# A two-layer encoder trunk on one core: work moved from the gap before attention into the values' phase

## The chip, the cores and the metric

The kernel runs on one core of a Trainium2 chip. Its time is device microseconds of one execution. TensorE (PE) multiplies matrices, VectorE (DVE), ScalarE (ACT) and GpSimd (POOL) do the elementwise work, and SyncE (SP) issues nearly all DMA transfers, one after the other and in the order of the program.

## The reference

The input is 1024 rows (frames) of 1024 numbers. Layer 0 mixes the rows with a gated MLP, layer 1 with attention over the own chunk of 64 rows and the eight before it; either ends with a gated feed-forward block. Cut to what this change touches:

```python
h = h + gmlp_mixer(rmsnorm(h, a_norm_g), ...)
h = h + conv_ffn(rmsnorm(h, f_norm_g[0]), ...)            # ffn(0), down(0)
kv = rmsnorm(h, kv_norm_g) @ w_kv                         # keys, values: 16 heads of 64
q = (rmsnorm(h, b_norm_g) @ w_q) * 64 ** -0.5
sc = q . k + rel_bias[clip(i - j)]                        # a chunk sees itself and the 8 chunks before it
o = softmax(sc) @ v
h = h + o @ w_o
h = h + conv_ffn(rmsnorm(h, f_norm_g[1]), ...)
out = rmsnorm(h, final_norm_g)
```

## The kernel before, in words

Everything is float32. An operand is split by a cast on ACT (or DVE) and a subtraction on DVE (or POOL) into a high and a low part, and a product is three matmuls: high by high, high by low, low by high. Large products are done in the Strassen manner: seven products of half-size blocks instead of eight, whose operands are sums of blocks.

The stretch around the change runs like this.

- **down(0)**, the second half of the first feed-forward block, does its seven products in the order 1, 6, 2, 7, 5, 4, 3, each in 11 steps of 12 matmuls; the operands of a step are loaded and split three steps ahead. Beside it, `value_sums` makes what the values need: for each of four k it loads two blocks of the values' weights (tile `vr`), multiplies them by the norm's gain on POOL (L1047, 128x1024 each), forms four block sums on POOL (tile `vS`, L383, 128x512 each) and stores those in DRAM. `aside` says at which step that is called. When products 6 and 7 end, POOL adds them into the residual stream (L960).
- **values()** makes V, again in seven products (1, 2, 3, 6, 7, 5, 4) of four steps m with 12 matmuls (L1139). It takes its weights from DRAM and its results go back there (`vhi`, `vlo`). After products 1 and 3 the queries and keys of the first pair of heads are projected (tile `qk`, L181/184/188), and before the change those results stay in PSUM until V is done.
- **The gap**: then the first pair's q and k are split (`first`), copied by DMA into the tiles that attention reads (`stage`: KM, QE, QS, KS, two rows of 64 partitions each, 12 DMAs for head 0 and 12 for head 1), and `constant_rows` brings constant rows from DRAM through a small tile `e` to the other 64 partitions. `Max` loads the head's bias, forms its row maxima (`mx` matmuls, L1286 and L1293, reduced on DVE at L1289 and L1295) and writes them as one more row into QE (`mr`, L1302 to L1306), so that a score comes out already less its maximum. The first score (`st`, L1332) waits for all of it. Meanwhile PE does START = 75 matmuls of the second pair's projection, the "fills".
- **The heads**: 16 heads by 8 key blocks, a loop of 128 steps s. A step does one block's scores, two blocks of the next head's maxima, the values' product (`po`) of two steps earlier, and some fills, which are the projections of later pairs until step 104, and then the output projection `wo`. `stage` brings the next head's rows.
- **The output projection**: `w_o` weights are loaded at the steps in `loads`; the last pair's result is normalised on DVE, split, and multiplied in.

The order of PE's instructions is written by hand: matmuls advance a clock of the program, and `put_off(us, fn)` issues `fn` when that clock has moved on by so much. The other engines are ordered by a scheduler, except in the first 24 steps of `down`, and each DMA of SP keeps its place in SP's order. An instruction that has to wait holds back what stands behind it on its engine.

## Time and profile before

| | us |
|---|---|
| median of 3 runs (lowest to highest) | 2194.47 (2192.28 to 2202.92) |
| the profiled execution: its time, its span | 2200.13, 2198.4 |
| PE busy | 2124.1 (97% of the span) |
| DVE, ACT, POOL busy | 1591.9, 1075.4, 802.0 (72%, 49%, 36%) |
| mean granted PE clock | 0.984 of full speed |
| values, gap, heads, output projection (from the timeline) | 937 to 1037, to 1087, to 1470, to 1500 |

In the views below, a timeline's row is the start, the duration, the engine, the line of the code, the operation, output<-inputs, and in square brackets the idle time before it and what ended that. L184 is line 184 of the kernel before. A row of the waits is engine, line and what it waited for, then the sum in us, how often, and the longest. A row of the windows gives for a stretch its length and then the busy time (and count of instructions) of PE, PEld, DVE, ACT and POOL, the granted PE clock, the share of the DMA engines and GB/s. Matmuls overlap: a row's duration (0.39 us) is longer than the distance of two starts.

### The profile page before, as it was taken

Reading aid. Unit: us, or ns where it says so; the run is one execution under the profiler, and the core shown is the slowest. Engines: PE = TensorE matmul, PEld = TensorE weight load, DVE = VectorE, ACT = ScalarE, POOL = GpSimd, SP = SyncE. Lnnn points to the kernel's source line nnn. Section 1 sums busy time; section 2 is a strip of 40 time slices with the busy share of each in tenths; the row PEclk is TensorE's granted clock in tenths of the full one; section 3 lists DMA queues with packets and bytes.
Section 4 is the critical chain, followed back from the end, with each engine's and each line's share of the span. In section 5 each row is a group of like instructions: output and inputs, shape, how many; then the busy total and the mean of one; then the engine's idle time right before and its main releaser. Section 6 shows DMA issues by size and latency. Waiting matters only on the chain.

```text
span 2198.4 us, 28916 instructions
## 1 busy us (share of the span) xinstructions
PE 2124.1 (97%) x9832; PEld 1770.0 (81%) x9832; DVE 1591.9 (72%) x2354; ACT 1075.4 (49%) x1879; POOL 802.0 (36%) x560
## 2 busy tenths in 40 slices
PE   9999999999999999999599999889999999999998
PEld 8888878888888878888487888768778888888887
DVE  4197889888888887786255655664888888876676
ACT  6423556454445535544355656542545545454443
POOL 1084743423335552133355544431223332441120
PEclk9999999999999999999799999999999999999999
DMA  7267622545447988444556656834234454579553
GB/s 250 76 211 261 241 78 92 180 142 175 155 152 241 351 296 277 172 134 145 150 130 162 168 136 156 230 115 145 95 110 168 137 185 134 190 245 331 192 188 138
DMA packets 220812, 391.99 MB, mean 178 GB/s; under 512 B 60764, under 2 KB 75484, under 8 KB 220664
## 3 DMA queue, kind: packets, MB, share of 16 engines
q1 hardware_dynamic: 217640, 384.69, 54.6%
q10 hardware_dynamic: 3024, 5.46, 0.7%
q8 instruction: 77, 1.26, 0.2%
q14 instruction: 71, 0.58, 0.1%
HBM read 248.85 MB, written 115.98 MB: 166 GB/s over the span
## 4 chain that ended last, share of the span: by engine, by line
PE 83%; DMA 6%; DVE 6%; issue 2%; POOL 1%; SPq 1%; ACT 1%; DVEq 0%; POOLq 0%; ACTq 0%
PE gate L992 8%; PE up L992 8%; PE up L370 7%; PE up L368 7%; PE up L373 7%; PE gate L373 5%; PE gate L370 5%; PE gate L368 5%; PE vps L503 4%; PE v L1139 3%; PE qkv L188 2%; PE qkv L181 2%; PE qkv L184 2%; PE ups L181 1%; PE ups L184 1%
## 5 line engine op out<-in xcount | busy, mean ns | idle before, releaser
L140 DVE TENSOR_TENSOR wlo<-raw,whi 128x512 fp32r<-128x512 f32 x380 | 349.2, 925 | 139.6 <-ACT whi L139 139.3
L139 ACT CAST whi<-raw 128x512 fp32r<-128x512 f32 x380 | 235.2, 622 | 286.9 <-PE gate L992 180.0
L368 PE MATMUL up<-yh,whi 128*128 128x512 f32 x688 | 268.3, 390 | 3.4 <-ACT whi L139 2.0
L370 PE MATMUL up<-yh,wlo 128*128 128x512 f32 x688 | 268.4, 390 | 0.3 <-DVE wlo L140 0.3
L840 POOL TENSOR_TENSOR h<-a 128x512 f32<-128x512 f32 x44 | 83.9, 1908 | 407.4 <-DVE a L832 394.8
L1346 POOL TENSOR_TENSOR pl<-p,ph 128x640 fp32r<-128x640 f32 (+4 forms) x128 | 159.8, 1251 | 165.2 <-ACT ph L1345 113.1
L370 PE MATMUL gate<-th,wlo 128*128 128x512 f32 x496 | 193.3, 390 | 0.0
L368 PE MATMUL gate<-th,whi 128*128 128x512 f32 x496 | 193.1, 389 | 0.0
L373 PE MATMUL up<-yl,whi 128*128 128x512 f32 x688 | 184.3, 390 | 0.0
L140 DVE TENSOR_TENSOR yl<-raw,yh 128x512 fp32r<-128x512 f32 x172 | 152.4, 888 | 9.0 <-ACT yh L139 9.0
L368 PEld LDWEIGHTS up<-yh,whi 128*128 128x128 f32 x688 | 129.1, 188 | 31.3 <-ACT whi L139 2.4
L370 PEld LDWEIGHTS up<-yh,wlo 128*128 128x128 f32 x688 | 129.3, 188 | 27.6 <-DVE wlo L140 1.1
L373 PEld LDWEIGHTS up<-yl,whi 128*128 128x128 f32 x688 | 129.2, 188 | 27.2 <-POOL yl L140 0.5
L373 PE MATMUL gate<-tl,whi 128*128 128x512 f32 x496 | 132.9, 390 | 0.2 <-DVE tl L140 0.2
L139 ACT CAST whi<-S 128x512 fp32r<-128x512 f32 x160 | 99.1, 619 | 65.8 <-PE up L373 59.8
L140 DVE TENSOR_TENSOR wlo<-S,whi 128x512 fp32r<-128x512 f32 x160 | 129.6, 811 | 0.0
L992 PE MATMUL up<-yl,whi 128*128 128x512 f32 (+1 forms) x312 | 121.7, 390 | 2.0 <-DVE yl L140 1.9
L992 PE MATMUL up<-yh,wlo 128*128 128x512 f32 (+1 forms) x312 | 120.9, 387 | 2.6 <-DVE wlo L140 2.6
L139 ACT CAST yh<-raw 128x512 fp32r<-128x512 f32 x190 | 115.1, 616 | 13.5 <-DMA raw<-gB 8.8
L992 PE MATMUL gate<-yh,wlo 128*128 128x512 f32 (+1 forms) x312 | 121.0, 388 | 0.0
L992 PE MATMUL gate<-yl,whi 128*128 128x512 f32 (+1 forms) x312 | 120.8, 387 | 0.0
L992 PE MATMUL up<-yh,whi 128*128 128x512 f32 (+1 forms) x312 | 120.8, 387 | 0.0
(328 smaller groups left out, 5420.4 us busy)
## 6 DMA issues: line engine op xcount, KB each, us to landing
raw<-in_f_win SPq DMA_DIRECT2D x88, 512.0 KB
gT<-h SPq DMA_DIRECT2D x88, 256.0 KB
h<-in_f_wdown SPq DMA_DIRECT2D x44, 512.0 KB
dS<-h SPq DMA_DIRECT2D x88, 256.0 KB
raw<-dS SPq DMA_DIRECT2D x40, 512.0 KB
raw<-gT SPq DMA_DIRECT2D x40, 512.0 KB
gB<-a SPq DMA_DIRECT2D x66, 256.0 KB
raw<-in_f_wdown SPq DMA_DIRECT2D x30, 512.0 KB
```

Of the source, the lines that this page charges most:

```text
L139: behind[S] = S.copy(hi, src)
L140: return eng.tensor_tensor(lo, src, f32(hi), op=ALU.subtract)
L181: nc.tensor.matmul(ps, wh[:, k, :], xs[k][0], start=k == first, stop=False)
L184: nc.tensor.matmul(ps, wl[:, k, :], xs[k][0], start=False, stop=False)
L368: nc.tensor.matmul(ps, wh[:, k, :], xs[k][0], start=first and k == 0, stop=False, skip_group_check=True)
L370: nc.tensor.matmul(ps, wl[:, k, :], xs[k][0], start=False, stop=False, skip_group_check=True)
L373: nc.tensor.matmul(ps, wh[:, k, :], xs[k][1], start=False, stop=k == 3, skip_group_check=True)
L503: nc.tensor.matmul(ps, a, b, start=k == i == 0, stop=k == KD - 1 and i == 2)
L840: G.tensor_tensor(B[n], x, B.get(y) if isinstance(y, str) else y, op=ALU.subtract)
L992: nc.tensor.matmul(ps[:, cs], w[:, ms], x[:, cs], start=q == i == 0 and p in (1, 6, 5, 4), stop=q == NP - 1 and i == 2, skip_group_check=True)
L1139: nc.tensor.matmul(bank[m], a, b, start=p not in (2, 7) and k == i == 0, stop=k == 3 and i == 2, skip_group_check=True)
L1346: marks[2] = G.tensor_tensor(pl[:, :n], pf[:, :n], f32(ph[:, :n]), op=ALU.subtract)
```

## The change

1. **The gap's work moves into the values' phase.** The first pair's q and k are split as soon as they are projected and written to DRAM (`part`, then 8 DMAs). From there the rows of head 0 are staged: KM and QE (`"me"`) right after each projection, QS and KS (`"s"`) at product 4. Head 0's constant rows are brought in 8 us after the start of the phase by the program's clock, its 15 `mx` matmuls and the row of maxima stand within products 7, 5 and 4 (`first_max`). What stays behind the last value is head 1's staging (12 DMAs) and head 1's constant rows.
2. **START falls from 75 to 56** fills before the first score. The weights of those fills are loaded within the values' phase.
3. **Buffers of the values' phase:** `vt` 4 to 3, `vx` 5 to 3, `vw` 8 to 6, PSUM's two held banks are given up.
4. **`value_sums` later in down(0):** called at steps 46, 53, 60, 67 instead of 28, 37, 46, 55, and POOL takes its multiplications only behind the additions L960.
5. **Bias in two halves** (one for scores, one for maxima), loaded up to a head earlier than before.
6. **Maxima a step sooner** in every head, and their row put off from step 5 instead of 6.
7. **Output projection:** all eight `w_o` weights are on chip before the heads end (two more, at steps 118 and 122, into tiles that are free by then), and the fills behind the last step are 14 instead of 12 per waiting value and reach over m = 7 and 6.

The core of the diff:

```diff
-START = 75
+START = 56
...
                     for x in ((h12,) if p == 6 else (h21, h22)):
-                        G.tensor_tensor(x, x, u, op=ALU.add)
+                        behind["adds"] = G.tensor_tensor(x, x, u, op=ALU.add)
...
-            G.tensor_tensor(rows[j], rows[j], cc[:, c:c + 1].broadcast_to([P, T]), op=ALU.mult)
+            with tc.issue_after(behind["adds"].ins):
+                G.tensor_tensor(rows[j], rows[j], cc[:, c:c + 1].broadcast_to([P, T]), op=ALU.mult)
...
-        down(0, gs, ds, hsave[0], lambda t, acc: norm(h, acc, t, X), {28 + 9 * k: lambda k=k: value_sums(k) for k in range(4)})
+        down(0, gs, ds, hsave[0], lambda t, acc: norm(h, acc, t, X), {46 + 7 * k: lambda k=k: value_sums(k) for k in range(4)})
...
-            if p in (2, 6) and m == 0:
+            if p in (2, 6, 4) and m == 0:
                 yield
...
+    parts = {(0, what): [dp.tile([P, T], F32, name=f"{what}0{n}") for n in ("hi", "lo")] for what in "qk"}
...
+    open_psum(H, 4)
+    with tc.tile_pool(name="vt", bufs=3, reuse_waits="tile") as vt, tc.tile_pool(name="vx", bufs=3, reuse_waits="tile") as vx, \
+            tc.tile_pool(name="vw", bufs=6, reuse_waits="tile") as vw:
+        w2 = {what: weights(0, what) for what in "qk"}
+        put_off(8.0, lambda: constant_rows(0, lambda: npl.tile([P, H], F32, tag="f", name="e")))
+        ys = [None] * 2
+
+        def first_max():
+            place = h_all[1, 1]
+            mx = Max(0, load_bias(1, 0, place[:, 0, 0:2 * P]), place[:, 1, 0:NB], place[:, 1, NB:2 * NB], lambda: mr0,
+                     lambda: place[:, 2, 0:2 * P])
+            for b in range(NB):
+                put_off(3.0 + 1.4 * b, lambda b=b: mx.block(b))
+            put_off(16.0, mx.row)
+
+        for t, _ in enumerate(values()):
+            if t == 2:
+                for hs in halves:
+                    stage(0, hs, "s")
+                continue
+            ys[t] = X["B11"] + X["B21"] if t == 0 else X["B12"] + X["B22"]
+            for what in "qk":
+                ps = psS("qk")
+                proj(ps, w2[what], ys[t])
+                both = [npl.tile([P, H], F32R, tag="acc", name=f"{what}{n}", bufs=4) for n in ("hi", "lo")]
+                part(what, *both, ps)
+                for d, a in zip(parts[0, what], both):
+                    nc.sync.dma_start(d[:, halves[t]], f32(a))
+            stage(0, halves[t], "me")
+            if t:
+                raw1 = new_raw([P, KD, P])
+                w1 = {what: weights(1, what, raw1) for what in "qk"}
+                put_off(12.0, first_max)
+        catch_up()
...
+        put_off(7.0, lambda: constant_rows(1, lambda: b2.tile([P, H], F32, tag="o", name="e")))
         for c in range(2):
-            constant_rows(c, lambda: b2.tile([P, H], F32, tag="o", name="e"))
...
-        mx = Max(0)
-        for b in range(NB):
-            put_off(6.5 + 0.8 * b, lambda b=b: mx.block(b))
-        put_off(14.0, mx.row)
+        bs, bm = {0: new_bias(0, 0)}, {1: new_bias(1, 1)}
...
-        loads = {100: 2, 102: 3, 106: 4, 109: 5, 112: 0, 116: 1}
+        loads = {100: 2, 102: 3, 106: 4, 109: 5, 112: 0, 115: 1, 118: 6, 122: 7}
...
-        mid, end = {2: (1,), 3: (3,), 4: (5,), 5: (7,)}, {1: (0,), 2: (2,), 3: (4,), 4: (6,)}
+        mid, end = {1: (1,), 2: (3,), 3: (5,), 4: (7,)}, {0: (0,), 1: (2,), 2: (4,), 3: (6,)}
...
             if i == LAG + 1 and hd + 1 < NH:
+                bs[hd + 1] = new_bias(0, hd + 1)
+                if hd + 2 < NH:
+                    bm[hd + 2] = new_bias(1, hd + 2)
                 stage_v(hd + 1)
...
-                if i == (6 if p < LAST - 1 else 5):
-                    put_off(0.5 if p < LAST - 1 else 2.0, mx.row)
+                if i == 5:
+                    put_off(0.5, mx.row)
...
-        fill = output([(m, range(LAST - 2, LAST), psS) for m in (2, 3, 4, 5)])
+        two = range(LAST - 2, LAST)
+        fill = output([(7, range(LAST), psS, True), *((m, two, psS, False) for m in (2, 3, 4)), (6, range(LAST), psO, False),
+                       (5, two, psS, False)])
         for h0, b in waiting:
-            for _ in range(12):
+            for _ in range(14):
                 next(fill)
```

Three places show what moves. Lines shift by the change: L1332 before is L1349 after (`st`), L1286 is L1196 (`mx`), L1213 is L1182 (staging), L1182 is L1158 (constant rows).

SP behind the last value before the change: the end of head 1's staging (`km_9394` and so on are head 1's tiles, `thi` and `tlo` the split q and k), the constant rows having been issued between the stagings:

```order
L1182 DMA e<-in_consts 64x512 x2
L1213 DMA km_9394<-thi 64x512
L1213 DMA qe_9392<-thi 64x512
L1213 DMA qs_9393<-thi 64x512
L1213 DMA qs_9393<-tlo 64x512
L1213 DMA ks_9395<-tlo 64x512
L1213 DMA ks_9395<-thi 64x512
L1267 DMA vh_9396<-vhi 128x8x64
L1267 DMA vl_9398<-vlo 128x8x64
L1276 DMA bias<-in_bias 128x512 x2
```

and the same place after, where 12 stagings of head 1 (from `q0hi` and the like in DRAM) begin right behind the last value:

```order
L1182 DMA ks_9469<-k0lo 64x512
L1182 DMA ks_9469<-k0hi 64x512
L1314 DMA vh_9470<-vhi 128x8x64
L1314 DMA vl_9472<-vlo 128x8x64
L1218 DMA bias<-in_bias 128x256 x2
L1158 DMA e<-in_consts 64x512 x2
L1218 DMA bias<-in_bias 128x256 x2
L1314 DMA vh_9471<-vhi 128x8x64
L1314 DMA vl_9473<-vlo 128x8x64
L156 DMA raw<-in_w_kv 128x1024
L1158 DMA e<-in_consts 64x512 x2
```

Head 0's rows have left this place; the two pairs of constant rows `e` that are left are head 1's, and stand behind its staging, two bias loads and V's first loads.

PE between the values and the scores, before (head 0's first maxima among the fills `qkv`):

```order
L184 MATMUL qkv<-yh,wlo 128x512
L181 MATMUL qkv<-yh,whi 128x512
L1286 MATMUL mx<-km_9352,qe_9350 128x128
L184 MATMUL qkv<-yh,wlo 128x512
L181 MATMUL qkv<-yh,whi 128x512
L184 MATMUL qkv<-yh,wlo 128x512
L1286 MATMUL mx<-km_9352,qe_9350 128x256
```

and after, at the end of 56 fills (head 0's first scores, then head 1's first maximum, whose tiles are `km_9468` and `qe_9466`):

```order
L184 MATMUL qkv<-yh,wlo 128x512
L1349 MATMUL st<-qe_8354,km_8356 128x256
L1351 MATMUL st<-qs_8355,ks_8357 128x256
L1349 MATMUL st<-qe_8354,km_8356 128x384
L1351 MATMUL st<-qs_8355,ks_8357 128x384
L181 MATMUL qkv<-yh,whi 128x512
L184 MATMUL qkv<-yh,wlo 128x512
L181 MATMUL qkv<-yh,whi 128x512
L184 MATMUL qkv<-yh,wlo 128x512
L181 MATMUL qkv<-yh,whi 128x512
L1196 MATMUL mx<-km_9468,qe_9466 128x128
```

The scores stand where the maxima stood; the first instruction that reads head 1's constant rows now comes five fills behind the first scores.

POOL in down(0), before (additions L960 between the third and the fourth set of value sums):

```order
L1047 TENSOR_TENSOR vr<-vr,cc 128x1024 x2
L383 TENSOR_TENSOR vS<-vr 128x512
L383 TENSOR_TENSOR vS<-vS,vr 128x512
L383 TENSOR_TENSOR vS<-vr 128x512
L383 TENSOR_TENSOR vS<-vr,vS 128x512
L960 TENSOR_TENSOR h_84<-h_84,u 128x512 x4
L1047 TENSOR_TENSOR vr<-vr,cc 128x1024 x2
```

and after:

```order
L960 TENSOR_TENSOR h_85<-h_85,u 128x512
L960 TENSOR_TENSOR h_86<-h_86,u 128x512
L1047 TENSOR_TENSOR vr<-vr,cc 128x1024 x4
L383 TENSOR_TENSOR vS<-vr 128x512
L383 TENSOR_TENSOR vS<-vS,vr 128x512
L383 TENSOR_TENSOR vS<-vr 128x512
L383 TENSOR_TENSOR vS<-vr,vS 128x512
```

All twelve additions now stand ahead of all the value sums.

199 lines of the change are left out of this document (89 added, 110 removed).

## The prediction

> **What bounds the kernel now.** First the page's busy times, then the waits of PE, then windows and timelines of the stretches that the diff touches.
>
> ```profile
> PE 2124.1 (97%) x9832; PEld 1770.0 (81%) x9832; DVE 1591.9 (72%) x2354; ACT 1075.4 (49%) x1879; POOL 802.0 (36%) x560
> ```
>
> PE is busy for 2124 of 2198 us, and the change leaves its products as they are. So only what PE stands still for, 74 us, and what it does at a slow clock can be won. The largest piece lies between the last value and the first score:
>
> ```profile
> 1037.01 0.39 PE L1139 MATMUL v<-vwh,vtl 128*128 128x512 f32 x1
> 1037.23 0.39 PE L181 MATMUL qkv<-yh,whi 128*128 128x512 f32 x1
> ...
> 1058.19 0.45 PE L1286 MATMUL mx<-km,qe 128*128 128x128 f32 x1 [13.77 <-DMA e<-in_consts]
> ...
> 1073.11 0.58 PE L1293 MATMUL mx<-km,qe 128*128 128x256 f32 x1 [9.68 <-DVE mb L1289]
> ...
> 1087.03 0.28 PE L1332 MATMUL st<-qe,km 128*128 128x256 f32 x1
> ```
>
> From 1037.23 to 1087.03 are 49.8 us. In them PE does 75 fills, one every 0.227 us (the distance of the first two rows), 17.0 us, and 15 maxima with 3840 columns, 1.7 us, with the row's transpose about 1.9. **The gap costs 49.8 - 18.9 = 30.9 us**, partly as idle time, partly as slow clock:
>
> ```profile
> 1045.00:1050.00 5.00, 0.00 (x0) 0.00 (x0) 0.00 (x0) 0.00 (x0) 4.90 (x6) 0.70 1.07 296
> 1060.00:1065.00 5.00, 3.44 (x11) 2.45 (x9) 0.29 (x1) 1.85 (x3) 1.03 (x2) 0.50 0.56 163
> 1075.00:1080.00 5.00, 4.06 (x15) 3.18 (x14) 4.10 (x8) 1.72 (x3) 1.90 (x1) 0.72 0.16 61
> 1080.00:1085.00 5.00, 4.12 (x19) 3.09 (x20) 2.75 (x9) 0.25 (x1) 0.00 (x0) 1.00 0.24 61
> ```
>
> The eighth column is the granted clock: half speed from 1050 to about 1077. What ends the waits is in the chain of waits:
>
> ```profile
> 1050.08 4.09 DMA e<-in_consts
> 1055.53 2.84 DMA e<-in_consts
> 1059.03 2.71 DMA e<-in_consts
> 1061.77 0.63 ACT qe L1183
> 1062.95 0.59 SPq L1213
> 1068.15 4.38 DMA bias<-in_bias
> ```
>
> Constant rows go through two small tiles, one pair after the other, each 2.7 to 4.1 us from issue to landing and 0.6 us for the cast; then SP issues head 1's staging, V's loads, and only then the bias, for which the maxima wait.
>
> **The gap after the change.** Head 0's staging, constant rows, maxima and bias are gone from it, so the first scores wait for 56 fills only (56 x 0.227 = 12.7 us, work that counts anyway). The 19 other fills are done later in the heads; that is no gain and no loss. But head 1's first maximum stands five fills and four score matmuls behind, at 61 x 0.227 + 0.6 = 14.4 us after the last value, and needs head 1's constant rows. I rebuild SP's order with the rows of before:
>
> ```profile
> 1041.50 0.83 SPq L1097 DMA_DIRECT2D vlo<-vl  x1
> 1061.38 1.52 SPq L1182 DMA_DIRECT2D e<-in_consts  x2
> 1063.59 0.59 SPq L1213 DMA_DIRECT2D qe<-thi  x1
> 1064.22 0.60 SPq L1213 DMA_DIRECT2D qs<-thi  x1
> 1068.15 1.29 SPq L1276 DMA_DIRECT2D bias<-in_bias  x2
> ```
>
> The last value's store is issued 4.5 us behind the last matmul. Then 12 stagings at 0.63 us (start to start): 12.1. Two loads of V: 13.4. Two biases, 1.3: 14.7. The first two constant rows at 14.7 to 16.2, landing 2.7 to 4.1 later, 0.6 for the cast: the first small tile is free at 18 to 19.5. Two biases and V's other two loads fill SP until 18.7, and q's next weight load stands there too. The second two rows, KM's, are issued at about 19 to 21, land at 22 to 25 and are cast by 23 to 25.5. So PE waits about **9 us** (8.5 to 11 by this sum, 6.5 if the store goes a little earlier and lands fast), and all later scores are behind it. After it comes slow clock. Its price is in the output projection:
>
> ```profile
> 1469.90 0.40 PE L184 MATMUL wo<-yh,yl 128*128 128x512 f32 x1
> ...
> 1477.53 0.77 PE L181 MATMUL wo<-yh,whi 128*128 128x512 f32 x1 [3.60 <-DVE h L1569]
> 1482.26 0.79 PE L184 MATMUL wo<-yh,wlo 128*128 128x512 f32 x1 [3.97 <-DVE wlo L140]
> ...
> 1486.69 0.63 PE L184 MATMUL wo<-yh,wlo 128*128 128x512 f32 x1
> 1487.12 0.52 PE L181 MATMUL wo<-yh,whi 128*128 128x512 f32 x1
> ```
>
> Behind these two waits matmuls start every 0.43 us from 1482.26 to 1487.12, 4.9 us in which 11 were done instead of 21: 2.3 us lost. So the gap costs 11.3 us afterwards; it gives 30.9 - 11.3 = 19.6.
>
> The Trainium skill ("TensorE: Matmul & The Clock Gate", Part 1: The HAM clock gate) says that the clock halves after an idle window of about 3.4 us and comes back after some 3.4 us of sustained work. Both stalls above agree with the first half; the second would be an estimate of 1.7 us instead of the 2.3 measured here. By the page the sum would be 0.6 us better.
>
> **The values' phase** takes the work over. It has PE idle for nothing:
>
> ```profile
> PE bc L210 <- ACT dg L209: 0.5, 1, 0.5
> ```
>
> That is all PE waited for between 905 and 1037. What comes in: 15 maxima and a transpose on PE (1.9 us, counted in the gap before), eight splits that had to be done anyway, and on SP 8 stores, 12 stagings, 4 constant rows, a bias and a row, 26 issues at 0.63 = 16 us, in a phase of 100 us. SP's queue is in order, and some of these wait for an engine; behind them stand the stores of V and the weight loads. With 6 weight tiles instead of 8 the third and fourth weights of a product can be loaded into their tiles only when the product before is in its last step, 12 x 0.227 = 2.7 us long. A late pair costs at most the landing and the split:
>
> ```profile
> L140 DVE TENSOR_TENSOR vwl<-raw,vwh 128x512 fp32r<-128x512 f32 x16 | 15.5, 994 | 3.8 <-ACT vwh L139 3.7
> ```
>
> 0.6 us of cast, 1.0 of subtraction, and 4.4 of landing (the bias above; the loads themselves are not bound to a tile). Cast and subtraction for the third weight have 6 matmuls (1.4 us) more before it is needed. So between 0 and 4 us in all; I take 1.5.
>
> **down(0).** Value sums on POOL hold up DVE. Three rows of DVE and two of POOL:
>
> ```profile
> 752.88 1.78 DVE L140 TENSOR_TENSOR yl<-raw,yh 128x512 fp32r<-128x512 f32 x1
> 783.22 0.68 DVE L958 TENSOR_TENSOR u<-up,s 128x512 f32<-128x512 f32 x1
> 837.74 0.69 DVE L140 TENSOR_TENSOR wlo<-raw,whi 128x512 fp32r<-128x512 f32 x1 [1.42 <-ACT whi L139]
> L1047 POOL TENSOR_TENSOR vr<-vr,cc x8: 2064/2336/2343, 745.9 to 792.1; 128x1024 f32<-128x1024 f32 x8
> L383 POOL TENSOR_TENSOR vS<-vr x8: 1617/1682/1742, 752.5 to 797.8; 128x512 f32<-128x512 f32 x8
> ...
> 780.00:790.00 10.00, 6.68 (x28) 4.67 (x26) 8.22 (x8) 2.29 (x4) 10.00 (x8) 1.00 1.08 373
> 790.00:800.00 10.00, 9.18 (x31) 6.83 (x32) 10.00 (x6) 3.52 (x6) 9.84 (x6) 0.83 0.83 290
> ```
>
> A split's subtraction takes 0.69 us alone and 1.78 beside POOL; the addition whose input lies in PSUM stays at 0.68. In the two windows PE did 59 matmuls, where 20 us hold 88: 6.6 us are lost, at the place where POOL's additions and sums meet. The change moves 8 x 2.3 + 16 x 1.7 = 46 us of POOL work in one block behind the last addition, to about 852 to 900. There DVE needs two subtractions per step of 2.7 us; held, they take 2 x 1.75 = 3.5, so it falls behind by 0.8 us a step, and with the products' additions (0.68 each, four to a product) by about 1.1, over 46 / 3.8 = 12 steps: 13 us. Three steps of lead swallow up to 8 of it, then the slow clock can add 2.3: 5 to 8. I take 8.6 against the 6.6 of before: **2 us lost**, and as bounds 6 lost (all 13) and 4 gained (the lead covers all but 2.6). On the rest of the engines nothing waits for these sums until product 2 of V.
>
> The Trainium skill ("GPSIMD Engine Reference", 1. Specifications) says that POOL shares its SBUF interfaces with DVE, and that DVE instructions with two SBUF inputs contend. The rows 1.78 and 0.68 agree. It speaks against packing the sums beside splits; it does not speak for either place, since both have them.
>
> **The heads.** PE's waits from the first score to the end of the loop:
>
> ```profile
> PE st L1332 <- DMA qe<-mr: 7.6, 5, 2.8
> PE st L1332 <- DVE mb L1289: 7.0, 4, 2.1
> PE po L1362 <- DVE o L1391: 3.2, 1, 3.2
> PE mr L1302 <- DVE mb L1297: 3.1, 3, 1.8
> 1396.50 7.92 DMA bias<-in_bias
> ```
>
> The row of maxima comes a step (3 us) sooner; its longest wait is 2.8, so the 7.6 go. The 3.2 are a bias that landed after 7.9 us and held DVE, which copies `o`; loaded up to a head sooner it is not late. The maxima's own waits (7.0 and 3.1: DVE behind with reductions) move with them and stay. Against it, the upper half of Q and K has 2.5 steps instead of 3.5 from staging to the maximum that reads it: six issues and a landing (3.8 + 4.1 = 7.9 of 7.5 us) are just late in the worst case. I book 10.8 less one such wait of 1.8: **9 us** gained; bounds 2 (each wait replaced by another) and 16 (the maxima's 3.1 and half of the 7.0 too, with their slow clock).
>
> **The output projection.** Between 1469.90 and 1487.12 stand the two waits above, 3.60 + 3.97, and the 2.3 of slow clock: 9.9 us. What ends them: DVE's normalisation and residual additions, then the split of the seventh weight. With all weights split before, and 66 matmuls instead of 24 to be issued there, both are covered; the same products simply stand elsewhere. But SP's loads of the second half's operands wait for the store of the last pair, and 12 of them at 0.63 us can come 0 to 3 us late. I take 1.4: **8.5 us**, bounds 5 (3 late, and 1.9 of waits that stay) and 9.9.
>
> **Sum.** Gap 19.6, values -1.5, down -2, heads 9, output 8.5: 33.6 us less. The profiled execution took 2200.13 us (span 2198.4), 5.7 above the median of the runs, 2194.47; the saving is taken off both, 2166.5 for an execution like that one, **2161 for the median**.
>
> **The rivals.**
>
> A. *The wait at head 1 replaces that at head 0.* SP's `e` pairs, one behind the other, stand for both heads in the rows above; if V's loads, the weights or the stores hold SP for 10 us more, head 1's maximum waits 19 instead of 9. Against it: nothing of head 0 is left in that queue. Price 10 and some 2 of slow clock: 2161 + 12 = 2173.
>
> B. *Everything is covered.* Head 1's rows land while PE still has fills, the lead swallows the sums in down, the heads gain 13. Gains 4 + 1.5 + 4 + 4 + 2 more: about 2145. For it, the idle DVE and ACT in the gap; against it, SP's 30 issues in line.
>
> C. *SP's queue starves V (slower).* Each of the six product changes waits in full: landing 4.4, cast 0.6, subtraction 1.0, then slow clock 2.3, in all 8.3; six make 50 us, and 2161 - 1.5 + 50 = 2209. For it: 26 new issues, waiting ones among them, ahead of just-in-time weights. Against it: PE waits nowhere there now, and the first two weights of a product come earlier. It decides from about 47 us, nearly all six; with three it is 2185.
>
> D. *The change doesn't do what it says in the heads*: rows come no sooner since DVE's reductions hold them, heads and output give only 2 and 5: 2172.
>
> **How the numbers follow.** Forecast 0.58 (alone 2150 to 2171), A 0.14, B 0.11, C 0.09 (half of it below 2205), D 0.08. About 0.5% (11 us) is what a measurement of this kernel can tell from no change: faster is below 2183.5, slower above 2205.4. Forecast, B and D are below, A for seven eighths, so 0.89, of which I take 0.02 off for several small misses at once: faster 0.87. C's half and the rest of A and the misses: same 0.08. C in full: slower 0.05. The range for 8 in 10 takes in A's and D's times and reaches to B and, on the other side, to the sum with gap, heads and output at their low bounds (2161 + 5 + 7 + 3.5 + 6): **2144 to 2183**.
>
> **What would show it.** Right: the first score 13 to 15 us behind the last value; one wait of `mx` on head 1's constant rows of 6 to 11 us and half clock after it; no wait of `st` for the row of maxima over 1 us in the heads; no wait above 2 us between the last `po` and the second half of the output projection; PE idle under 2 us in the values' phase; DVE's splits at 1.78 us around 852 to 900. Wrong: waits of PE on V's weights at product changes (C), two waits of over 8 us before the second block of scores (A), or a stretch in down with over 15 us lost.

## The result, and the profile after

The changed kernel takes 2183.62 us (median of 7 runs, 2176.0 to 2186.22), the kernel before 2199.31 us in runs beside it (7, 2192.28 to 2202.92): a ratio of 0.9932, 95% interval 0.9910 to 0.9953. It is faster by 0.7%, 15 us. 33.6 us were forecast, and 2183.62 lies just above the range that was given (2144 to 2183).

The profiled execution of the changed kernel took 2186.06 us, its span is 2184.3 us, 14.1 less than before. Where they come from shows in what PE loses per stage. The loss of a stage is its time on the timeline of PE less the time its matmuls take back to back at full clock (0.227 us for 512 columns, 0.176 for 384, 0.118 for 256, 0.108 for 128, the usual distance of two starts), so idle time and slow clock together; half clock for 3.4 us counts as 1.7 us. In the table, "before, again" is a second profile of the kernel before, taken for an experiment below; its span is 2186.3 us, so single executions of one kernel differ by 12 us.

| loss of PE, us | before | before, again | after | change forecast | change measured (against the two) |
|---|---|---|---|---|---|
| down(0) | 8.4 | 9.1 | 14.9 | +2 | +6.5, +5.8 |
| values | 1.2 | 1.2 | 10.7 | +1.5 | +9.5, +9.5 |
| last value to end of head 4 | 38.6 | 33.7 | 20.0 | -19.6 and a part of the heads | -18.6, -13.7 |
| heads 5 to 16 | 32.8 | 26.3 | 23.1 | most of -9 | -9.7, -3.2 |
| last `po` to end of the output projection | 10.8 | 11.1 | 8.7 | -8.5 | -2.1, -2.4 |
| all the rest | 15.5 | 13.8 | 15.9 | 0 | +0.4, +2.1 |

The waits of PE after (engine, line, what it waited for: us in all, times, longest):

```profile
PE mx L1196 <- issue: 15.1, 1, 15.1
PE up L992 <- DVE yl L140: 4.6, 9, 1.0
PE mr L1211 <- ACT p L1359: 3.9, 1, 3.9
PE wo L181 <- DMA oh<-osave: 2.7, 6, 0.6
...
PE v L1141 <- DVE vwl L140: 2.4, 1, 2.4
PE up L992 <- ACT yh L139: 2.3, 1, 2.3
PE bc L210 <- ACT dg L209: 2.1, 1, 2.1
```

The waits for `e<-in_consts` (13.8) and for the bias behind it (9.7) are gone; one of 15.1 us stands in their place, and waits in down (`up`), in the values (`v`, `bc`) and behind the heads (`oh<-osave`) are new.

**The gap.** PE's timeline, then SP's and ACT's:

```profile
1054.99 0.39 PE L1141 MATMUL v<-vwh,vtl 128*128 128x512 f32 x1
...
1068.13 0.28 PE L1349 MATMUL st<-qe,km 128*128 128x256 f32 x1
...
1085.14 0.45 PE L1196 MATMUL mx<-km,qe 128*128 128x128 f32 x1 [15.11 <-issue]
```

```profile
1062.12 0.32 SPq L1099 DMA_DIRECT2D vlo<-vl  x1
1062.54 1.89 SPq L1182 DMA_DIRECT2D km<-k0hi  x1
...
1070.86 0.59 SPq L1182 DMA_DIRECT2D ks<-k0hi  x1
...
1074.07 1.12 SPq L1158 DMA_DIRECT2D e<-in_consts  x2
...
1078.91 1.11 SPq L1158 DMA_DIRECT2D e<-in_consts  x2
```

```profile
1084.43 1.14 ACT L1159 CAST km<-e 64x512 fp32r<-64x512 f32 x2 [4.97 <-DMA e<-in_consts]
```

The first score starts 13.1 us behind the last value. The first maximum of head 1 starts 30.1 us behind it, once the first half of the second pair of constant rows (KM's) is cast. The row "issue" names no releaser, but PE starts 0.1 us after the first of these two casts ends. The last store of V is issued 7.1 us behind the last matmul, not 4.5, and the first staging takes 1.89 us, not 0.63; from there the rows run nearly as in the working. The second pair is issued 23.9 us behind the last value (19 to 21 in the working), and its cast starts 5.5 us later.

The late store has a row on DVE: before it can write the next low part of V's results, DVE waits for an earlier store of such a part to land.

```profile
1058.30 1.77 DVE L140 TENSOR_TENSOR vl<-c,vh 128x512 fp32r<-128x512 f32 x1 [2.88 <-DMA vlo<-vl]
```

In the kernel before, DVE waits for no store behind the last value.

**The values.** The chain of waits near 958 and the windows around it:

```profile
950.02 2.59 DMA e<-in_consts
...
952.64 0.61 ACT km L1159
...
953.89 0.62 ACT km L1159
...
954.53 0.73 ACT vwh L1081
...
956.26 1.39 POOL st L200
...
957.67 1.29 ACT dg L209 x4
```

```profile
956.00:958.00 2.00, 0.90 (x4) 0.40 (x3) 1.37 (x4) 1.19 (x4) 1.74 (x2) 1.00 0.46 96
...
960.00:962.00 2.00, 2.00 (x5) 1.28 (x4) 1.08 (x3) 0.17 (x1) 0.00 (x0) 0.50 0.40 72
```

ACT waits for head 0's constant rows to land, V's weight casts stand behind them, and the norm of the second half behind those: PE is idle for 2.1 us and then runs at half clock. Near 985 PE waits 2.4 us for the low part of a weight of V (`vwl`), where DVE has been busy for 19.91 of 20 us. The first row is the window after, the second the same place of the phase before:

```profile
965.00:985.00 20.00, 18.29 (x81) 14.81 (x79) 19.91 (x26) 8.20 (x15) 10.88 (x8) 1.00 0.48 171
```

```profile
956.00:976.00 20.00, 20.00 (x90) 16.57 (x89) 19.89 (x26) 8.09 (x15) 12.68 (x9) 1.00 0.25 87
```

DVE was as full before, and PE waited for nothing. What differs is how early the weights are ready. The third product reads its four weights from 972 on before and from 982 on after. The split of the fourth stands at 949.80 before; after, those of the third and fourth come only just in time (DVE before; DVE and PE after):

```profile
949.80 1.82 DVE L140 TENSOR_TENSOR vwl<-raw,vwh 128x512 fp32r<-128x512 f32 x1 [0.48 <-ACT vwh L139]
```

```profile
984.97 1.88 DVE L140 TENSOR_TENSOR vwl<-raw,vwh 128x512 fp32r<-128x512 f32 x3
```

```profile
985.70 0.50 PE L1141 MATMUL v<-vwl,yh 128*128 128x512 f32 x1 [2.42 <-DVE vwl L140]
```

Counted over the phase, every weight was ready 9.8 us or more ahead of its first matmul before the change. After it the third and fourth weights of four of the seven products are ready 0.05 to 3 us ahead. In all PE waits 5.9 us in the values, and half clock behind the waits of 2.1 and 2.4 us costs 3.4 us more; these 9.3 us are nearly the whole 10.7.

**down(0).** DVE's subtractions stay long from 850 to 873 and again from 884 to 895, and one load, `raw<-gT`, is issued late, 8.6 us behind the one before it, and takes 6.39 us to land (DVE's timeline, then the chain of waits, then PE's timeline):

```profile
855.46 2.38 DVE L140 TENSOR_TENSOR wlo<-raw,whi 128x512 fp32r<-128x512 f32 x1
...
871.95 1.78 DVE L140 TENSOR_TENSOR yl<-raw,yh 128x512 fp32r<-128x512 f32 x1
```

```profile
875.52 6.39 DMA raw<-gT
```

```profile
884.06 0.80 PE L992 MATMUL up<-yh,whi 128*128 128x512 f32 x1 [2.28 <-ACT yh L139]
```

Of the 14.9 us, 6.3 are PE's waits for splits on DVE (4.6 and 1.7), 2.3 the wait for that load, and about 3 the half clock behind it (0.50 from 884 to 888, 0.67 to 892).

**Behind the heads.** The waits for `wlo` and `h` are gone. The loads of the second half's operands come one by one, and the clock falls to half for 10 us (windows of 4 us, the last ends at 1486):

```profile
1474.00:1478.00 4.00, 2.17 (x7) 0.99 (x6) 2.84 (x5) 0.63 (x1) 0.00 (x0) 0.97 1.00 290
1478.00:1482.00 4.00, 3.27 (x7) 1.65 (x6) 0.00 (x0) 0.00 (x0) 0.00 (x0) 0.50 1.02 378
1482.00:1486.00 4.00, 4.00 (x15) 3.42 (x15) 0.16 (x1) 0.01 (x1) 1.03 (x1) 0.50 1.01 340
```

The DMA engines are busy all the time (shares 1.00 to 1.02): 256 KB every 0.68 us, the distance of SP's issues there, is what they do here.

### The profile page after: what moved, and what is told of

The parts are those of the page before. It is cut to its first block, busy times and chain, and to the rows that moved or that the text cites. A ratio compares the mean times of both kernels' runs of the same rounds, so it can differ in the third digit from the quotient of the medians.

```text
span 2184.3 us, 28950 instructions
## 1 busy us (share of the span) xinstructions
PE 2127.6 (97%) x9832; PEld 1770.1 (81%) x9832; DVE 1606.0 (74%) x2355; ACT 1076.2 (49%) x1879; POOL 798.5 (37%) x560
## 4 chain that ended last, share of the span: by engine, by line
PE 83%; DVE 9%; DMA 3%; issue 3%; ACT 1%; SPq 1%; POOL 0%; DVEq 0%; POOLq 0%; ACTq 0%
PE up L992 8%; PE gate L992 8%; PE up L370 7%; PE up L368 7%; PE up L373 7%; PE gate L373 5%; PE gate L368 5%; PE gate L370 5%; PE vps L503 4%; PE qkv L181 2%; PE qkv L188 2%; PE qkv L184 2%; DVE wlo L140 2%; PE v L1141 2%; DVE yl L140 2%
## 5 line engine op out<-in xcount | busy, mean ns | idle before, releaser
L140 DVE TENSOR_TENSOR wlo<-raw,whi 128x512 fp32r<-128x512 f32 x378 | 344.4, 917 | 150.3 <-ACT whi L139 149.9
L992 PE MATMUL gate<-yh,whi 128*128 128x512 f32 (+1 forms) x312 | 120.5, 386 | 0.0
```

The lines of the kernel that those rows point to most:

```text
L140: return eng.tensor_tensor(lo, src, f32(hi), op=ALU.subtract)
L992: nc.tensor.matmul(ps[:, cs], w[:, ms], x[:, cs], start=q == i == 0 and p in (1, 6, 5, 4), stop=q == NP - 1 and i == 2, skip_group_check=True)
```

## The experiments

All are edits of the changed kernel unless said otherwise. "Ratio" is to the kernel before, in runs on the same chip, with its 95% interval; the changed kernel has 0.9932. Most single edits move the ratio by less than the interval is wide, so the stages' losses of one profile each are read beside it. Those scatter too. The runs of the changed kernel whose edit leaves a stage alone have 14.0 to 17.6 us in down, 8.4 to 10.7 in the values, 18.3 to 20.1 to head 4, 20.1 to 25.7 in heads 5 to 16, and 4.2 to 9.2 behind the last `po`.

| run | ratio | down | values | to head 4 | heads 5 to 16 | behind last `po` |
|---|---|---|---|---|---|---|
| the change | 0.9932 | 14.9 | 10.7 | 20.0 | 23.1 | 8.7 |
| e_rows_first | 0.9936 (0.9911 to 0.9960) | 15.0 | 9.7 | 15.4 | 24.2 | 8.1 |
| e_rows_bias_first | 0.9917 (0.9894 to 0.9939) | 14.0 | 9.7 | 10.3 | 24.3 | 7.7 |
| e_start75 | 0.9955 (0.9936 to 0.9974) | 16.6 | 8.4 | 17.8 | 20.5 | 9.0 |
| e_vw5_vt4 | 0.9981 (0.9968 to 0.9995) | 14.1 | 22.4 | 13.8 | 20.5 | 9.0 |
| e_no_low | 0.9948 (0.9927 to 0.9969) | 17.6 | 7.3 | 18.5 | 25.7 | 7.8 |
| e_rows0_later | 0.9949 (0.9930 to 0.9968) | 16.9 | 10.2 | 18.6 | 23.4 | 8.9 |
| e_direct | 0.9938 (0.9918 to 0.9958) | 15.9 | 8.0 | 14.1 | 22.3 | 7.7 |
| e_sums_back | 0.9930 (0.9907 to 0.9953) | 9.1 | 9.5 | 18.7 | 21.9 | 8.1 |
| e_loads_early | 0.9948 (0.9933 to 0.9964) | 15.3 | 9.5 | 20.1 | 21.0 | 9.0 |
| e_residual_later | 0.9938 (0.9917 to 0.9960) | 14.8 | 10.4 | 18.3 | 20.1 | 5.9 |
| e_max_late | 0.9942 (0.9921 to 0.9963) | 15.5 | 9.6 | 20.0 | 19.6 | 9.2 |
| e_bias_late | 0.9941 (0.9918 to 0.9964) | 14.6 | 9.8 | 19.1 | 19.7 | 4.2 |
| e_both_late | 0.9941 (0.9920 to 0.9963) | 14.8 | 10.6 | 19.9 | 21.7 | 4.4 |
| e_heads_before | 0.9930 (0.9905 to 0.9954) | 17.3 | 10.7 | 19.2 | 17.4 | 7.9 |
| the kernel before, again | 0.9988 (0.9969 to 1.0007) | 9.1 | 1.2 | 33.7 | 26.3 | 11.1 |
| e_all | 0.9863 (0.9839 to 0.9888) | 8.5 | 10.2 | 9.9 | 22.4 | 2.6 |
| e_three_max_late | 0.9861 (0.9839 to 0.9882) | 9.1 | 9.4 | 12.9 | 20.0 | 2.5 |
| e_three_direct | 0.9854 (0.9829 to 0.9878) | 8.6 | 8.0 | 7.6 | 23.1 | 2.6 |

### The gap

Theory: head 1's constant rows hold PE, as the last thing in SP's queue that a maximum needs. Rival: the queue as a whole does, and whatever is put last decides.

```diff
-        put_off(7.0, lambda: constant_rows(1, lambda: b2.tile([P, H], F32, tag="o", name="e")))
...
+        constant_rows(1, lambda: b2.tile([P, H], F32, tag="o", name="e"))
         for hs in halves:
             stage(1, hs)
```

> The changed kernel, with head 1's constant rows issued ahead of its 12 stagings instead of behind them. Theory 1 (the constant rows alone hold PE after the values): the rows are issued some 10 us sooner, the one wait of the first maximum of head 1, 15.1 us in the changed kernel, falls below 4 us, no other wait of over 3 us takes its place in the first 30 us of the heads, and the loss between the last value and the end of the fourth head falls by 13 to 17 us; time about 2168. Theory 2 (all of SP's queue is the limit: whatever comes last in it decides): the wait passes to the two biases, which now stand behind the stagings, shown as PE waiting for DVE's maxima or for the first value product; 6 to 10 us of the 15 stay, time about 2176.

The one wait became three (waits from 1050 to 1180; `p` in the second row waits for the bias, which SP issues at 1076.27):

```profile
PE st L1348 <- ACT p L1358: 3.5, 1, 3.5
PE mx L1196 <- DVE p L1354: 3.5, 1, 3.5
PE mx L1196 <- ACT km L1159: 2.7, 1, 2.7
```

The loss falls by 4.6 us, not by 13. The same with the two biases moved ahead as well:

```diff
         open_psum(H, 2)
+        bs, bm = {0: new_bias(0, 0)}, {1: new_bias(1, 1)}
+        constant_rows(1, lambda: b2.tile([P, H], F32, tag="o", name="e"))
         for hs in halves:
             stage(1, hs)
         stage_v(0)
-        bs, bm = {0: new_bias(0, 0)}, {1: new_bias(1, 1)}
```

> As the run with the constant rows first, and the two biases (head 0's for scores, head 1's for maxima) ahead of them too; only the stagings of head 1 and V's loads stay behind. Theory 1: no difference to the run before it, time about 2168. Theory 2: this one is the better of the two by 4 to 8 us, since nothing that the first scores and maxima need is left behind the stagings; the remaining waits are V's loads, below 4 us; time about 2168 against 2176.

The loss falls by 9.7 us to 10.3, and two waits are left, 2.9 us for `p` and 2.4 for the cast. The rival holds: the order of all of SP's queue is what counts, and what the first scores and maxima need has to come ahead of the ten stagings that they don't need yet.

Whether fills cover that wait:

```diff
-START = 56
+START = 75
```

> The changed kernel with 75 fills before the first score, as before the change. Theory 1 (the wait for head 1's constant rows is a fixed time after the last value, and fills ahead of it are free): the 19 fills cover 4.3 us more of it, the wait of the first maximum falls from 15.1 to about 10.8 us and the loss of the first four heads from 20 to 15.5; the heads' other loss stays. Theory 2 (the fills' weights and evictions compete with the rows): the wait falls by less than 2 us.

The wait falls to 10.5 us, by 4.6, as the first theory says; the loss to head 4 by only 2.2, and the ratio is no better. And why SP was late (the expectation calls `vt` V's result tiles; it holds split operands of V, while the results `vh` and `vl` have four tiles in every kernel here):

```diff
-    with tc.tile_pool(name="vt", bufs=3, reuse_waits="tile") as vt, tc.tile_pool(name="vx", bufs=3, reuse_waits="tile") as vx, \
-            tc.tile_pool(name="vw", bufs=6, reuse_waits="tile") as vw:
+    with tc.tile_pool(name="vt", bufs=4, reuse_waits="tile") as vt, tc.tile_pool(name="vx", bufs=3, reuse_waits="tile") as vx, \
+            tc.tile_pool(name="vw", bufs=5, reuse_waits="tile") as vw:
```

> The changed kernel, with five weight tiles of V instead of six and four instead of three sets of V's result tiles. Theory 2 of the run before (weight tiles make the weights late): one tile less makes it worse, the waits of V's matmuls for weights grow from 2.8 to over 6 us and the loss in the values from 10 to 14 us or more; theory 1: below 12. At the end of the values: if three result tiles are what holds SP there (a low part waits for a store of 4.6 us to land), the last store of V is issued 4 to 5.5 us behind the last matmul instead of 7.1, and the first maximum of head 1 waits 12 to 13.5 us instead of 15.1; if not, both stay.

```profile
1064.34 0.39 PE L1141 MATMUL v<-vwh,vtl 128*128 128x512 f32 x1
```

```profile
1066.91 0.32 SPq L1099 DMA_DIRECT2D vlo<-vl  x1
```

The last store is issued 2.6 us behind the last matmul instead of 7.1, DVE waits for no store at that place, and the wait is 10.3 us instead of 15.1. In the 17 profiles of the changed kernel with three `vt` and six `vw` the last store comes 6.8 to 7.2 us behind, each time with a wait of DVE of 2.6 to 3.1 us for a store. That wait stands in the chain that makes SP late. What took it away here is not shown: the fourth set of operands, the fifth weight tile, or the values themselves, which ran slower in this run and gave the stores time to land.

### The values

That run shows the weights as well: with one tile less the loss in the values is 22.4 instead of 10.7 us. Six tiles leave no reserve. There is no run with eight, as before the change. The load on DVE:

```diff
-                part(what, *both, ps)
+                if what == "q":
+                    S.mul(both[0], ps, 0.125)
+                else:
+                    S.copy(both[0], ps)
+                G.memset(f32(both[1]), 0.0)
```

> The changed kernel, with the low parts of the first pair's q and k not formed: POOL writes zeros in place of the four subtractions on DVE (0.68 us each) that the change put into the values' phase, so the first two heads are computed from the high parts alone. It tells what fills the values' phase. Theory 1 (DVE has no time left between 965 and 985, where two of these subtractions stand among the sums and splits for V): the wait of V's matmuls for their weight's low part, 2.4 us near 983, falls below 1.2 us and the loss in the values from 10 to 7 us. Theory 2 (the weights are late because six tiles instead of eight let no weight be made ahead): wait and loss stay within 1 us.

The wait for the weights' low parts is 1.8 us in two pieces instead of 2.4 in one, the loss 7.3 instead of 10.7: between the two theories in the wait, with the first in the loss. Against the scatter of 8.4 to 10.7, four subtractions on DVE, 2.7 us of work, cost PE 1 to 3 us. The constant rows on ACT:

```diff
-        put_off(8.0, lambda: constant_rows(0, lambda: npl.tile([P, H], F32, tag="f", name="e")))
+        put_off(30.0, lambda: constant_rows(0, lambda: npl.tile([P, H], F32, tag="f", name="e")))
```

> The changed kernel, with head 0's constant rows put off 30 instead of 8 us into the values' phase by the program's clock: on ACT their casts then stand behind the norm's diagonal (dg) instead of ahead of it. Theory 1 (ACT waits for the constant rows to land and so holds V's weight casts and the second norm, and PE the norm's broadcast): the wait of bc for dg (2.1 us) and the slow clock behind it (2 us) go; the loss in the values falls from about 10 us to 6. Theory 2 (that wait comes from the load of work on DVE in general): it stays within 1 us of 10.

The norm's wait is gone (0.3 us), and V waits for the weight casts instead, which now stand behind the rows:

```profile
PE v L1141 <- DVE vwl L140: 2.5, 1, 2.5
PE v L1141 <- ACT vwh L139: 2.2, 1, 2.2
```

The loss stays (10.2): the wait has only changed its place in ACT's queue. So the casts were taken out of the phase, rounded once ahead of the first feed-forward block and kept in DRAM:

```diff
+                nc.sync.dma_start(a[oth], consts[oth, off + hs.start:off + hs.stop])
+                S.copy(b[oth], a[oth])
+                nc.sync.dma_start(cr[c][n][oth, hs], f32(b[oth]))
     gs, ds = ffn(0, X)
...
-            for hs in halves:
-                e = places()
-                nc.sync.dma_start(e[oth], consts[oth, off + hs.start:off + hs.stop])
-                S.copy(tl[oth, hs], e[oth])
+            nc.sync.dma_start(f32(tl[oth]), cr[c][n][oth])
```

> The changed kernel with the constant rows rounded once at the start of the program and kept in DRAM, and copied into Q's and K's tiles by one DMA each, with no small tile and no cast on ACT in between. Theory 1 (the casts in ACT's queue hold V's weight casts and the norm in the values' phase; two small tiles one behind the other hold the gap): the loss in the values falls from 10.7 to about 7 us, since PE waits neither for dg nor for vwh near 958, and the wait of the first maximum of head 1 falls from 15.1 to 8 or 9 us. Theory 2 (ACT and DVE are simply full in the values' phase): its loss stays at 9.5 to 11 us; the gap falls all the same.

```profile
PE mx L1203 <- DMA km<-cr: 9.6, 1, 9.6
```

The loss in the values is 8.0 and that to head 4 14.1, 2.7 and 5.9 less. Both waits on ACT are down to 0.3 us: head 0's constant rows in ACT's queue were the cause of those waits. The loss in the values is only 0.4 us below the lowest of the runs that leave it alone, so what those waits cost there is between 0.4 and 2.7 us. And the time is no better (0.9938), since the loss ahead of down(0) rises from 10.0 to 15.6 us in this profile: the eight casts and sixteen DMAs have a price where they stand now.

### down(0), and behind the heads

```diff
-            with tc.issue_after(behind["adds"].ins):
-                G.tensor_tensor(rows[j], rows[j], cc[:, c:c + 1].broadcast_to([P, T]), op=ALU.mult)
+            G.tensor_tensor(rows[j], rows[j], cc[:, c:c + 1].broadcast_to([P, T]), op=ALU.mult)
...
-{46 + 7 * k: lambda k=k: value_sums(k) for k in range(4)}
+{28 + 9 * k: lambda k=k: value_sums(k) for k in range(4)}
```

> The changed kernel, with the value sums called where they were before (steps 28, 37, 46, 55, and not behind the additions). Theory 1 (POOL's sums in one block, behind the additions, hold DVE's splits until PE starves): the loss in down(0) falls from 14.9 us to the 8.4 of the kernel before, the time by about 6 us to 2177. Theory 2 (the other rearrangements of this phase, the loads of V's first weights, cause the loss): it stays above 12 us.

9.1 us, as the first theory says: putting the sums later costs 5.8 us and earned nothing in the values (9.5 us with the sums back). How the 5.8 divide between slow splits on DVE and the late load is not shown, since the edit takes both away.

```diff
+            if s == 123:
+                for k in range(2):
+                    load_o(k, 1, None, [(QS, KS)[k][0][:, hs] for hs in halves])
...
-        for k in range(KD):
-            load_o(k, 1, wop, [(QS, KS)[k][0][:, hs] for hs in halves] if k < 2 else None)
+        for k in range(2, KD):
+            load_o(k, 1, wop)
```

> The changed kernel, with the first two of the eight operand pairs of the output projection's second half loaded at step 123 of the heads, into the tiles that are free since step 120, instead of behind the last head. Theory 1 (the loads in that stretch run at the limit of the DMA engines, 0.68 us for each 256 KB, and PE takes them one by one): 4 of 16 loads less, so the six waits for them (2.7 us) and the slow clock behind them (some 5 us) go nearly: the loss between the last po and the end of the output projection falls from 8.7 to below 4 us. Theory 2 (the loads are late because the store of the last pair and the residual's loads stand ahead of them in SP): the two early pairs don't help the other six, which still start at the same time, and the waits stay at 2 us or more.

This told nothing: the changed kernel's SP issues these four loads ahead of the last store already (at 1423 to 1433 of its timeline), so the edit moved no load. It serves as a second measurement of the change: 0.9948 where the first was 0.9932.

```diff
+                            with tc.issue_after(behind["o"].ins):
-                            nc.sync.dma_start(h[k][:, halves[1]], hsave[1][k, :, halves[1]])
+                                nc.sync.dma_start(h[k][:, halves[1]], hsave[1][k, :, halves[1]])
```

> The changed kernel, with the residual's eight loads for the second half issued behind the last load of the output projection's operands; before, three of them stand ahead (1.4 us of issue, 0.75 MB). Theory 1 (the loads run at the limit of the DMA engines, 0.68 us each, and PE takes them as they land): the operands come 1.5 to 2 us sooner, PE's waits for them fall from 2.7 to 1 to 2 us, and part of the slow clock stays; the loss behind the last po falls from 8.7 to 5 to 7 us. Theory 2 (they are bound by something else, the store of the last pair or the space): no change above 1 us.

The waits fall from 2.7 to 1.8 us, the loss from 8.7 to 5.9, as the first theory says. Neither is clear of the scatter: in runs that leave this stage alone the waits are 1.7 to 3.2 us and the loss 4.2 to 9.2. Together with the other edits it is 2.5 or 2.6 in three runs, below all of these; PE's clock stays full there, and behind the single edit it does not. So that the edit earns something is likely, and not shown.

### The heads

```diff
-        mid, end = {1: (1,), 2: (3,), 3: (5,), 4: (7,)}, {0: (0,), 1: (2,), 2: (4,), 3: (6,)}
+        mid, end = {2: (1,), 3: (3,), 4: (5,), 5: (7,)}, {1: (0,), 2: (2,), 3: (4,), 4: (6,)}
...
-                if i == 5:
-                    put_off(0.5, mx.row)
+                if i == (6 if p < LAST - 1 else 5):
+                    put_off(0.5 if p < LAST - 1 else 2.0, mx.row)
```

> The changed kernel, with the maxima and their row at the steps of the kernel before (a step later), all else changed, the early bias included. Theory 1 (the step earned what the heads gained): PE's waits of scores for the row of maxima, 0.7 us in the changed kernel, come back to about 7 us and the loss in heads 5 to 16 rises from 23 to 30 us or more. Theory 2 (the early bias earned it): they stay below 3 us, the loss at 23 to 26.

The waits for the row are back at 4.3 us, and the loss is 19.6, not 30: others went in exchange. Which ones shows over all profiles. With the early maxima the transpose that makes the row waits instead, for ACT as the profile puts it, 2.9 to 5.0 us in each of 14 profiles (`mr` for `p` above, 3.9 us, near the end of head 13), and in none of the six with the late ones, the two before included. Scores still wait for the row in most of these 14, 0.2 to 5.1 us in 12; the 0.7 us of the profile above is at the low end.

```diff
             if i == 0 and hd + 1 < NH:
+                if hd:
+                    bm[hd + 1] = new_bias(1, hd + 1)
+                    bs[hd + 1] = new_bias(0, hd + 1)
                 mx = new_max(hd + 1)
...
-                bs[hd + 1] = new_bias(0, hd + 1)
-                if hd + 2 < NH:
-                    bm[hd + 2] = new_bias(1, hd + 2)
+                if not hd:
+                    bs[1] = new_bias(0, 1)
```

> The changed kernel, with both halves of a head's bias loaded at the first step of the head before it, as late as in the kernel before, and the maxima a step sooner as in the changed one. Theory 1 (the early bias earned what the heads gained): the loss in heads 5 to 16, 23 us in the changed kernel and 33 in the one before, rises to 28 or more, with waits for the bias on DVE of several us again. Theory 2 (the maxima's step or the new order of the loads earned it): it stays at 20 to 25 us and DVE waits less than 2 us for a bias behind head 1.

No wait for a bias comes back behind head 1, and the loss is 19.7. Both at once:

> The changed kernel with both at once: the maxima at the steps of the kernel before, and both halves of the bias loaded at the first step of the head before. Alone, neither took anything back (loss in heads 5 to 16 of 19.6 and 19.7 us, 23.1 with both of the change's edits, 32.8 before). Theory 1 (either of the two is enough for the heads' gain): with both undone the loss comes back to 29 us or more. Theory 2 (the gain comes from something else, such as the more even fills or the order of the loads): it stays at 19 to 25 us.

21.7 us. Then, beside both, the staging behind the bias again (`with tc.issue_after(behind["bias"].ins)` around `stage(hd + 1, halves[1])`), and the kernel before a second time:

> The changed kernel with the maxima late, the bias late, and the staging of the next head's upper half behind the bias, as in the kernel before. Theory 1 (that order in SP's queue is what the heads gained by): the loss in heads 5 to 16 rises to 29 us or more from the 21.7 of both late. Theory 2 (no): it stays at 19 to 26 us.

> The kernel before once more, for how far one profile of it stands for others. In the profile shown, PE loses 32.8 us in heads 5 to 16, 10.8 behind the last po, 8.4 in down, 1.2 in the values, 30.8 between the last value and the first score. Theory 1 (the heads' loss of 32.8 is the kernel's): 30 to 35 us again. Theory 2 (it swings from execution to execution, as it does among the changed kernels, 19.6 to 25.7): it lies at 25 to 29 us, and the heads gained less than the two profiles say.

17.4 us, and 26.3 for the kernel before, where its first profile has 32.8 (its waits for the row are 4.0 us in this one and the 3.2 us behind a late bias 0.4). The changed kernels whose heads were not edited have 20.1 to 25.7. So the heads' loss of one kernel swings by 6 us from one execution to another, and none of the three edits earned anything that shows over that. What the change gained there, 3 to 10 us by its first profile and 1 to 13 by all of them, stays without a cause.

### Together

> Four of these edits at once on the changed kernel: biases and constant rows of head 1 ahead of the stagings, value sums where they were, head 0's constant rows put off, the residual's loads behind the operands'. If the four losses are separate places, the gains add: 9.6 us in the first heads, 6 in down, 4 in the values, 2 behind the last po, 21 us less than the changed kernel: about 2162 where the changed one has 2184, a ratio of 0.984 to 0.987 to the kernel before. If they cover one another (a gain in one place is given back in the next), it stays at the best single one, a ratio of about 0.991.

> The run of the four edits, without the later constant rows of head 0 (which earned nothing) and with the maxima back at the steps of the kernel before (which cost nothing). If the maxima's step is worth nothing or less, as the run with late maxima has it (loss in heads 5 to 16 of 19.6 us against 23.1), this is as fast as the four edits or up to 4 us faster: ratio 0.984 to 0.987 to the kernel before. If the step matters once the other waits are gone, it is 4 to 8 us slower, with PE's waits for the row of maxima at 4 us or more: ratio 0.988 to 0.990.

> Biases and constant rows of head 1 ahead of the stagings, value sums where they were, the residual's loads behind the operands', and the constant rows from DRAM without casts. If the gains add as in the run of the four edits (ratio 0.9863), and the casts are worth 4 us in the values and 3 in the gap, the ratio is 0.981 to 0.984; if the casts are worth nothing, 0.985 to 0.988.

The first is 2161.84 us (median of 4), the second, without the later constant rows and with late maxima, 2160.18, the third, with the rows from DRAM, 2160.44: ratios of 0.9863, 0.9861 and 0.9854, all with intervals below that of the change. The gains of separate places add in the main: down, the gap, and behind the heads give 6.4 + 10.1 + 6.1 = 22.6 us in the losses of the first, where the single edits gave 5.8 + 9.7 + 2.8 = 18.3, and the ratio falls by 0.7%, 15 us. The ratios of the single edits, 0.9917 to 0.9955 but for the slower run with five weight tiles, do not stand clear of the change's own interval; those of the edits together do. The three are not told apart, and the casts of the constant rows are worth nothing in sum, their 2 us in the values and in the gap being paid ahead of down(0) (12.1 us there against 9.1).

## Why the prediction was wrong

Against the profile that the forecast was worked out from, the gap and the heads together gave 28.3 of the 28.6 us that were forecast for them. What is missing lies in three terms: the values (8.0 us), the output projection (6.4) and down(0) (4.5), 18.9 us in all. That the first two came out so near is in part luck: against the second profile of the kernel before they gave 16.9 us.

**The gap, -19.6.** Right in the mechanism and nearly in its place: first scores at 13.1 us (12.7 and what stands between), one wait of `mx` on head 1's constant rows, half clock behind it. Wrong in the sum: "the last value's store is issued 4.5 us behind the last matmul" was read from the kernel before; after the change DVE waits for a store there, and it is 7.1. The first staging took 1.89 us instead of 0.63. The second pair's landing was taken from 2.7 to 4.1 and took 5.5. The wait was 15.1 instead of 9; half clock behind it, to 1088.6, cost 1.7 instead of 2.3. The loss to head 4 fell by 14 to 19 us. Rival A, SP held for 10 us more and a wait of 19, was half true.

**The values, +1.5.** The step that failed: 10.7 us instead of 1.2 and then 2.7. The prediction saw that six tiles let the third and fourth weights of a product be loaded only late, and that is what happened. But "a late pair costs at most the landing and the split" took the split at 1.6 us, cast and subtraction back to back. The cast was done by 982.6, and the subtraction started at 984.97, behind other work in DVE's queue. That DVE was full in this place mattered only now, since before the weights were split 24 us ahead. With the moved subtractions gone (e_no_low) the loss falls by 1 to 3 us, with one tile fewer (e_vw5_vt4) it grows by 12. The prediction also left out that ACT would stand still for constant rows (a wait of 2.1 us on PE; e_direct takes it away), and that half clock followed these two waits (3.4 us). Rival C named the place, waits for V's weights at product changes, and a price, but SP as the cause; PE waited for DVE and ACT.

**down(0), +2.** Right in sign, 6 instead of 2. The term was mis-sized already in the sum: the working gives 5 to 8 us, and 8.6 was taken. The splits were slow where it said (1.78 us, and 2.38 beside the multiplications). Left out were the moved DMAs: the stores of the sums wait for POOL in SP's queue (3.1 us), and a load of down behind them was issued late, a wait of 2.3 us on PE with half clock behind it. The bound of 6 lost ("all 13") was reached.

**The heads, -9.** The size lies within what was measured (3.2 and 9.7), the reasons do not hold, so it is right by luck. The row's 7.6 us of waits went in this profile (0.7 are left), but the transpose waits 3.9 us in their place, and putting the row back costs nothing (e_max_late); so for the bias. Waits that were seen once, in one profile, were added up as if each would be earned. The second profile of before has 4.0 us for the row and 0.4 behind the late bias.

**The output projection, -8.5.** Right that both waits are covered; wrong that little comes in their place. "12 loads can come 0 to 3 us late", 1.4 taken: 2.7 us of waits came, which the bound held. The step that failed is the slow clock behind them, put at nothing: half clock for 10 us, 5 us lost. In e_bias_late and e_both_late waits as long (2.8 and 3.1 us) came without it, and the stage lost 4.2 and 4.4.

**The rest.** No effect elsewhere was forecast and none shows above the scatter. Faster, with 0.87, came true by little: the mark for it was 0.5% (2183.5 us), and the kernel is 0.7% faster in runs beside the kernel before. No rival gives 2184; parts of several came at once.

## What to carry to other kernels

Work that is moved out of a gap into a stage where PE never waits does not come free because the engines that feed PE have idle time on average: look at the busy share of each helper in the very 20 us where it goes, and at what its queue, which is in order, will wait for. Look also at how long ahead of its use each operand is ready: a full helper cost nothing while the weights were split 24 us ahead, and 2.4 us of waiting once buffers were given up. In a long queue, order by who waits first: here six transfers (two biases, four of constant rows) put ahead of stagings that nothing needs yet took 9.7 of the 20.0 us lost up to the end of head 4. And a wait that is seen once in one profile is a sample: a second profile of the kernel before costs one run, and would have put a scatter of 6 us beside a gain of 9.

## What the runs showed of the clock

Short waits can halve PE's clock, and need not. Near 958 one wait of 2.1 us was enough (0.50 in the window from 960). In the kernel before, a wait of 2.06 us that ended at 1289.01 was followed by half clock (0.50 from 1290 to 1294), and waits of 2.00 us (to 1338.60) and 2.80 us (to 1396.70) were not (1.00 in the 4 us behind each). Behind the heads the same pattern, five or six waits of about 0.6 us, each with some 0.7 us of work between, left the clock at 0.50 for 10 us in the changed kernel and at 1.00 in the run with the late bias:

```profile
1468.00:1472.00 4.00, 2.43 (x8) 0.89 (x6) 3.34 (x6) 0.91 (x2) 0.00 (x0) 1.00 1.05 393
1472.00:1476.00 4.00, 2.79 (x15) 2.03 (x15) 0.00 (x0) 0.00 (x0) 0.00 (x0) 1.00 1.05 395
1476.00:1480.00 4.00, 4.00 (x20) 3.35 (x20) 2.12 (x5) 0.83 (x2) 1.02 (x1) 1.00 1.01 311
```

PE's waits are 2.8 us there and 2.7 in the changed kernel; the losses of the stage are 4.2 and 8.7. The Trainium skill ("TensorE: Matmul & The Clock Gate", Part 1: The HAM clock gate) gives an idle window of about 3.4 us for the fall of the clock, and says that the window runs freely. The free-running window agrees with the same waits giving half clock in one execution and not in the other; an idle time of 3.4 us without a break was not needed in either of the two places. In the clock records of both traces the stretches at 0.50 last 3.4 us or a multiple of it (the one at the program's end apart), for example 958.9 to 962.3 and 1477.7 to 1488.0 after the change, which fits a window of that length.
